# Three edits to the order of loads and sums in a two-layer SwiGLU and attention kernel

## The chip, the cores and the metric

The kernel runs on one core of one Trainium2 chip. The metric is the device time of one execution in microseconds (us). Three executions of the kernel before took 2139.57, 2142.0 and 2146.55 us; the median is 2142.0 us. A further execution was recorded by the hardware profiler, and every row of a profile in this document comes from such a recorded execution.

TensorE is called PE in the profile (PEld is its weight load), VectorE is DVE, ScalarE is ACT, GpSimd is POOL and SyncE, which only issues transfers here, is SP. "L448" is line 448 of the kernel.

## The reference, cut to what matters

One step of an encoder layer over 1024 prompt tokens and 32 sample tokens, 1024 features wide, all in float32:

```python
x = x + 0.5 * swiglu(rms_norm(x, ffn1_norm), ffn1_w_in, ffn1_w_out)   # "layer 0" here
h = rms_norm(x, mix_norm)
# eight stick-breaking attention heads of 64 and four HGRN2 heads of 128 from h @ w_in
sb_o = rms_norm(sb_mix(sq, sk, sv), sb_out_gain)                      # per head
o_h  = rms_norm(o_h, hg_out_gain) * silu(hg)                          # per head
x = x + concat(sb_o, o_h) @ w_out
x = x + 0.5 * swiglu(rms_norm(x, ffn2_norm), ffn2_w_in, ffn2_w_out)   # "layer 1" here

def swiglu(x, w_in, w_out):
    a, b = jnp.split(x @ w_in, 2, axis=-1)        # 1024 -> 2 x 2816
    return (jax.nn.silu(a) * b) @ w_out           # 2816 -> 1024
```

The outputs are the new activations, the new keys and values, and the new HGRN2 states.

## The kernel before, in words

**Stages.** The program is one straight line of instructions in five stages. By the profile's times they are: layer 0's first product (up to 486 us), layer 0's second product (486 to about 700 us), the mixing stage with attention and HGRN2 (to about 1440 us), layer 1's first product (to 1906 us) and layer 1's second product. Every float32 product is made of three passes of PE over a high and a low part of each operand (`PASSES`, `split`), and each feed-forward product is done with seven block products in place of eight (a Strassen-Winograd form). So the weights have to be summed and subtracted (S1 to S4) and split before PE reads them.

**The first product, `first_products`.** It loops over 22 columns `j` of 128 features, and in each over two halves `c` of the tokens (256 and 272 wide). A half is a list of block products `p`, each 12 matmuls on PE into one of eight PSUM banks, followed by an addition on DVE (L591), and for p = 4 and p = 3 a multiplication on POOL (L629 and L625) with a SiLU on ACT between (L624). The first `early` columns (6 in layer 0, 8 in layer 1) have had two of their products done ahead, so their halves have five products, in the order 6, 5, 7, 4, 3. Their parts come back from DRAM in tiles `fp` (`fetch`, L578). While column `j` runs, the weights of column `j + 1` are loaded (`wraw` and `braw`, L469 and L477), summed on DVE (`rS`, L496 to L499) and split in the second half (`S2l`, `S1l`, `S3l`, `A22l`, `S4l`, L159), each right behind the product that last used its buffer. At the end of a half POOL makes a difference `tt` (L563) that SP stores (`td<-tt`, L649), and at the end of a column SP stores `gd<-gt` (L650).

**The sums of the second weights, `out_sums`.** Beside this, once per column in the early columns, at p = 5 of the second half, the kernel loads a raw piece of the second weights in two transfers on SP (`oraw`, L545), makes four sums of it on POOL (`osum`, L549 to L552) and stores them (`sd<-osum`, L553) for the second product. There is one buffer for `oraw` and one for `osum`. The load and the sums stand in `with behind(g, last, stored)`: what SP issues in there comes behind the store of the column before (`stored`), and what POOL does comes behind its last multiplication L629 (`last`).

**The second product, `Second`.** It walks seven products with 11 steps `k` each. Weights come in pieces of two steps: `load_w` issues for each piece a transfer of the raw left operand (`rw`, for p = 1), one of the raw weights (`oraw2`, seen as `oraw`) and whatever `self.bulk` lists for that piece; all of it is issued by SP in that order (`move`, L708). The bulk lists hold the operands of later products: B22 (`qB`, needed from step 12 on) in four parts at pieces 2 to 5, T at 7 to 10, B21 at 12 to 15, and parts of x. `roomy` is false in layer 0 and true in layer 1. The split of a piece is L741 on ACT and L742 on DVE, that of a left operand L756 and L757; the matmuls are L800. The last column's stores go through POOL's own queue (`store = nc.gpsimd`), in both layers.

**The norms in the mixing stage.** `token_factors` squares a head's output, transposes it with PE (`pmc`, L218), sums it on DVE with a tensor_reduce (L219), and takes it to the power -1/2 on POOL (L224, L225). `spread` then widens the factor on ACT (`wide`, L237) and transposes it back with PE (`pb`, L245), and DVE multiplies (L1153 and L1518). PE does the projection of the next heads in between (`pp`, L939).

**What sets the order.** The order of instructions on each engine is not the order of the text. A planner runs through a model of the program and gives each engine the ready instruction with the highest priority; the place in the text is the priority, `high_priority()` raises it, and `behind(...)` fixes an instruction behind another one on the same engine. On the chip every engine then works strictly in that order. The planner doesn't know how long a transfer really takes.

Of the kernel before, what the change touches and what calls it, by code (L numbers as in the profile page):

```python
# [12 lines left out]
ALU = mybir.AluOpType  # L13
AX = mybir.AxisListType
# [6 lines left out]
TP = 1024  # L21
TS = 32
T = TP + TS
GROUPS = ((0, 384), (384, 768), (768, T))
NG = len(GROUPS)
TG = 384
# [181 lines left out]

def token_factors(g, f, psp, sq, w, behind_, tokens=None):


    nc = g.nc
    nb, rows, nh = -(-w // P), min(w, P), f.shape[2]
    mc = psp.tile([P, 3, P], F32, name="pmc", tag="px", bufs=3)
    v = f[0:rows, 0:nb, 0:nh]
    with behind(g, behind_):
        for b in range(nb):
            nc.tensor.transpose(mc[0:rows, b, :], sq[:, b * P:b * P + rows], g.ident)  # L218
    nc.vector.tensor_reduce(out=v.rearrange("p b h -> p (b h)"),  # L219
                            in_=mc[0:rows, 0:nb, :].rearrange("p b (h d) -> p (b h) d", h=nh), axis=AX.X, op=ALU.add)  # L220
    wide = lambda t: t[:, :, None].broadcast_to([rows, nb, nh])
    if tokens is not None:
        nc.gpsimd.tensor_tensor(out=v, in0=v, in1=wide(g.r2[0:rows, tokens]), op=ALU.mult)
    nc.gpsimd.tensor_scalar(out=v, in0=v, scalar1=nh / P, scalar2=EPS, op0=ALU.mult, op1=ALU.add)  # L224
    nc.gpsimd.tensor_tensor(out=v, in0=v, in1=g.mh[0:rows, :, None].broadcast_to([rows, nb, nh]), op=ALU.pow)  # L225
    if tokens is not None:
        nc.gpsimd.tensor_tensor(out=v, in0=v, in1=wide(g.rc[0:rows, tokens]), op=ALU.mult)
# [310 lines left out]

def out_sums(g, pool, w_out, sd, q, h):

    nc = g.nc
    v = w_out[0].rearrange("(f j p) (e d) -> p j f e d", f=2, p=P, e=2)
    raw = pool.get("oraw").rearrange("p (f e d) -> p f e d", f=2, e=2)
    for f in range(2):
        nc.sync.dma_start(raw[:, f], v[:, q, f, :, 256 * h:256 * h + 256])  # L545
    s = pool.get("osum").rearrange("p (i d) -> p i d", i=4)
# [9 lines left out]
def first_products(g, psp, pool, sizes, xs, wts, w_out, gd, td, sd, pd, early, sec, between=None):  # L556
# [3 lines left out]
    stored = added = silu = mm = last = None  # L560
    n_out = 0
    halves = [(q, h) for q in range(FH) for h in range(2)]
# [8 lines left out]
    def fetch(n):  # L571
        j, c = divmod(n, 2)
        if j < early:
# [5 lines left out]
            firsts[j, c] = t  # L579

    for n in range(2):
        fetch(n)
    for j in range(FC):
        n_halves = min(len(halves), j + j // 12 + j // 16 if early < 8 else j + 1 + j // 12)
        gt = gt_of(j)
        store = nc.gpsimd if j == FC - 1 else nc.sync
        for c in range(2):
# [13 lines left out]
            for i, p in enumerate(order):  # L601
# [40 lines left out]
                if (j, c, p) == (FC - 1, 1, 6):  # L642
                    sec.first_weights()
                if p == 5 and n_out < n_halves + c - 1:
                    with behind(g, last, stored):
                        out_sums(g, post, w_out, sd, *halves[n_out])
                    n_out += 1
            sub(tt, gt[:, ROLE[1], cc], tt if j >= FH else gt[:, ROLE[0], cc])
# [10 lines left out]
class Second:  # L659
# [23 lines left out]
    def open(self, psp, qpool, ring, pool, t_first):  # L683
# [15 lines left out]
        for i in range(4):  # L699
            k, e = 3 * i, min(3 * i + 3, FH)  # L700
            for n, at in (("B22", 2), ("T", 7), ("B21", 12)):
                self.bulk[at + i].append((self.q[n][:, k:e], src[n][:, k:e]))
# [436 lines left out]

def sb_out_norm(g, pool, psp, o, w, out):  # L1140
    nc = g.nc
    f = {}

    def factors(c):
# [3 lines left out]
        f[c] = pool.tile([P, 3, 2], F32, name="fo", tag="fo", bufs=3)  # L1148
        token_factors(g, f[c], psp, sq, cw, g.filler)

# [25 lines left out]
def attend_stream(g, m, pool, psp, gi, out):  # L1176
# [87 lines left out]
    while gi == 3 and not m.projected:  # L1264
        yield None
    yield from sb_out_norm(g, pool, psp, o, TP, out)
    m.attended[gi] = True
# [7 lines left out]
def sample_stream(g, m, pool, psp, gi, ck, cv, out):  # L1275
# [66 lines left out]
    while gi == 3 and not m.projected:  # L1342
        yield None
    yield from sb_out_norm(g, pool, psp, os, TS, lambda a, e, o: out(TP, T, o))
    m.sampled[gi] = True
# [61 lines left out]
def hg_stream(g, m, pool, psp, hh, state, outs, out):  # L1407
# [99 lines left out]
    def factors(n):  # L1507
# [5 lines left out]
        fo[n] = pool.tile([P, 3, 1], F32, name="fh", tag="fh", bufs=3)  # L1513
        token_factors(g, fo[n], psp, sq, TG, g.filler)

# [558 lines left out]
```

## Time and profile before

| what | value |
|---|---|
| median of three runs | 2142.0 us (2139.57 to 2146.55) |
| the profiled execution's own time | 2145.02 us |
| its span, first to last instruction | 2143.3 us |
| PE busy in the span | 2101.9 us (98%) |
| DVE, ACT, POOL busy | 1466.2, 935.4, 596.7 us |
| mean share of the granted TensorE clock | 0.999 |

The profiled execution is 3.0 us longer than the median of the runs and lies inside their spread. 1.7 us of its time lie outside the span. A wait in the profile is the idle time of an engine before an instruction, with what ended it. PE has next to none; the other engines are idle for about a third of the span or more.

### The profile page before, as it was taken

What the parts mean: (1) busy time and instruction counts of PE and PEld (TensorE: products, weight loads), DVE (VectorE), ACT (ScalarE), POOL (GpSimd) and SP (SyncE); (2) the same over time, 40 slices, a digit from 0 to 9 for tenths busy, and PEclk for the clock granted to TensorE, in tenths of its full rate; (3) what the DMA queues carried; (4) which work ended last, traced back from release to release, by engine and by line L of the source; (5) the groups of instructions that cost most, each with busy time, mean ns of one, the idle gap of its engine ahead of it and who ended that gap; (6) DMA issues with size and microseconds to landing.
All of it is one profiled execution on the core that took longest, in us unless ns stands there. A gap on an engine that the chain in (4) does not pass through costs nothing. (4 is left out here: it accounts for less than half of the span.)

```text
span 2143.3 us, 41511 instructions
## 1 busy us (share of the span) xinstructions
PE 2101.9 (98%) x16331; PEld 2049.2 (96%) x16331; DVE 1466.2 (68%) x2555; ACT 935.4 (44%) x1830; POOL 596.7 (28%) x878
## 2 busy tenths in 40 slices
PE   8999999999999999999999999999999999999999
PEld 8999999999999999899899898999999999999998
DVE  6776666654678568678678688568667666645775
ACT  6433332324447555564464564245233233334443
POOL 2455554530000201311312311031555454320000
PEclk9999999999999999999999999999999999999999
DMA  7765455538545310111211213555665455566343
GB/s 239 220 206 164 148 166 167 173 126 304 185 129 170 99 44 20 61 54 30 70 42 32 69 54 96 175 170 181 213 192 186 155 173 163 162 228 234 121 145 126
DMA packets 326085, 305.12 MB, mean 142 GB/s; under 512 B 26049, under 2 KB 281793, under 8 KB 325889
## 3 DMA queue, kind: packets, MB, share of 16 engines
q1 hardware_dynamic: 258896, 264.23, 37.9%
q10 hardware_dynamic: 66368, 36.08, 5.9%
q8 instruction: 128, 2.10, 0.4%
q0 software_dynamic: 624, 2.15, 0.3%
q14 instruction: 69, 0.56, 0.1%
HBM read 207.37 MB, written 95.03 MB: 141 GB/s over the span
## 5 line engine op out<-in xcount | busy, mean ns | idle before, releaser
L800 PE MATMUL bk<-tl,wh 128*128 128x256 f32 x1144 | 325.8, 285 | 1.8 <-DVE tl L757 1.8
L800 PE MATMUL bk<-th,wh 128*128 128x256 f32 x1144 | 323.5, 285 | 1.2 <-ACT th L756 1.2
L800 PE MATMUL bk<-th,wl 128*128 128x256 f32 x1144 | 323.0, 283 | 0.0
L939 PE MATMUL pp<-xs_a,wh 128*128 128x384 f32 (+1 forms) x1008 | 258.6, 338 | 0.0
L800 PEld LDWEIGHTS bk<-tl,wh 128*128 128x128 f32 x1144 | 215.7, 189 | 2.5 <-DVE tl L757 2.4
L800 PEld LDWEIGHTS bk<-th,wl 128*128 128x128 f32 x1144 | 216.6, 189 | 0.2 <-issue 0.2
L800 PEld LDWEIGHTS bk<-th,wh 128*128 128x128 f32 x1144 | 214.7, 189 | 1.9 <-ACT th L756 1.7
L939 PEld LDWEIGHTS pp<-xs_a,wh 128*128 128x128 f32 x1008 | 168.6, 189 | 6.0 <-issue 4.1
L939 PE MATMUL pp<-xs_a,wl 128*128 128x384 f32 (+1 forms) x504 | 164.0, 325 | 0.0
L742 DVE SCALAR_TENSOR_TENSOR wl<-oraw,wh 128x1024 fp32r<-128x1024 f32 x78 | 89.3, 1145 | 96.3 <-ACT wh L741 96.3
L624 ACT ACTIVATE gt<-gt 128x256 f32<-128x256 f32 x88 | 37.3, 423 | 261.4 <-DVE gt L591 261.1
L625 POOL TENSOR_TENSOR gt<-gt,b 128x256 f32<-128x256 f32 x88 | 70.8, 804 | 285.4 <-ACT gt L624 285.3
L741 ACT ACTIVATE wh<-oraw 128x1024 fp32r<-128x1024 f32 x78 | 77.7, 996 | 135.7 <-PE bk L800 115.1
L448 PE MATMUL bk<-ops_a,wh 128*128 128x256 f32 (+1 forms) x704 | 130.7, 286 | 2.0 <-ACT e L427 2.0
L159 DVE TENSOR_TENSOR wl<-wraw,wh 128x512 fp32r<-128x512 f32 (+2 forms) x126 | 111.6, 901 | 28.0 <-ACT wh L158 27.7
L158 ACT ACTIVATE wh<-wraw 128x512 fp32r<-128x512 f32 (+2 forms) x126 | 89.5, 731 | 75.4 <-PE pp L939 25.2
L448 PEld LDWEIGHTS bk<-ops_a,wh 128*128 128x128 f32 x704 | 109.0, 188 | 3.2 <-ACT e L427 3.1
L591 DVE TENSOR_TENSOR b<-bk,u 128x272 f32<-128x272 f32 (+1 forms) x176 | 75.4, 428 | 49.1 <-POOL gt L625 26.3
L448 PE MATMUL bk<-ops_a,wl 128*128 128x272 f32 (+1 forms) x352 | 100.0, 285 | 0.2 <-DVE wl L159 0.2
L629 POOL TENSOR_TENSOR gt<-gt,b 128x256 f32<-128x256 f32 x88 | 85.6, 973 | 43.0 <-DVE b L591 32.5
L939 PEld LDWEIGHTS pp<-xs_a,wl 128*128 128x128 f32 x504 | 94.8, 188 | 0.1
L591 DVE TENSOR_TENSOR gt<-bk,p 128x256 f32<-128x256 f32 (+1 forms) x60 | 26.0, 433 | 96.0 <-PE bk L448 91.5
(461 smaller groups left out, 6675.6 us busy)
## 6 DMA issues: line engine op xcount, KB each, us to landing
wraw<-in_ffn_w_in_dram SPq DMA_DIRECT2D x58, 512.0 KB, 4.2
oraw<-in_ffn_w_out_dram SPq DMA_DIRECT2D x94, 256.0 KB, 4.7
sd<-osum SPq DMA_DIRECT2D x44, 512.0 KB, 3.2
gd<-gt SPq DMA_DIRECT2D x42, 528.0 KB, 5.0
braw<-in_ffn_w_in_dram ACTq DMA_DIRECT2D x42, 512.0 KB, 4.6
oraw<-sd SPq DMA_DIRECT2D x40, 512.0 KB, 3.7
oraw<-in_ffn_w_out_dram SPq DMA_DIRECT2D x30, 512.0 KB, 3.7
wraw<-in_w_in_dram SPq DMA_DIRECT2D x28, 512.0 KB, 3.7
```

Source lines behind the costliest of these rows:

```text
L158: high = nc.scalar.activation(hi, src, AF.Copy)
L159: nc.vector.tensor_tensor(out=lo, in0=src, in1=hi, op=ALU.subtract)
L448: mm = g.nc.tensor.matmul(ps, wt[x][:, kk, :], xt[y][:, kk, :], start=(first and kk == 0 and n == 0), stop=(kk == HK - 1 and n == len(PASS ...
L591: add = lambda out, other: nc.vector.tensor_tensor(out=out, in0=ps, in1=other, op=ALU.add)
L624: silu = nc.scalar.activation(gt[:, 1, cc], gt[:, 1, cc], AF.Silu)
L625: nc.gpsimd.tensor_tensor(out=gt[:, 1, cc], in0=gt[:, 1, cc], in1=s["b2"], op=ALU.mult)
L629: last = nc.gpsimd.tensor_tensor(out=gt[:, 0, cc], in0=gt[:, 0, cc], in1=s["b1"], op=ALU.mult)
L741: nc.scalar.activation(h, r, AF.Copy, scale=0.5)
L742: nc.vector.scalar_tensor_tensor(out=l, in0=r, scalar=0.5, in1=h, op0=ALU.mult, op1=ALU.subtract)
L800: nc.tensor.matmul(ps, wt[a][:, d * P:(d + 1) * P], xt[b][:, cols(c)], start=(k == 0 and n == 0), stop=(k == FH - 1 and n == len(PASSES) - 1))
L939: g.filler = nc.tensor.matmul(ps[:, 0:gw(n)], wt[a][:, k, :], xs(b, k)[:, gs(n)], start=(k == 0 and j == 0), stop=(k == KC - 1 and j == le ...
```

## The change

Three edits, and a rewriting of a count.

1. `out_sums` is parted in two: `out_load` (the two transfers L545) and the sums. In layer 1 (`early == 8`) the first piece is loaded ahead of column 0, and those of columns 1 to 7 at p = 7 of the column's first half, outside of `behind`. The sums stay at p = 5 of the second half, behind `last` and `stored`. In layer 0, and from column 8 on, load and sums stay together as before. `due(n)` gives the same number of pieces at each half as the expression that it replaces.
2. In layer 0 the four parts of B22 are listed at pieces 3 to 6, and no longer at 2 to 5. Layer 1 keeps 2 to 5.
3. In `token_factors` the tensor_reduce L219 gets high priority, for the norms of the attention's heads and of the HGRN2 heads of groups 0 to 2; those of group 3 pass `urgent=False`. The factors of q and k had high priority already.

No instruction is added or taken away.

```diff
-def token_factors(g, f, psp, sq, w, behind_, tokens=None):
+def token_factors(g, f, psp, sq, w, behind_, tokens=None, urgent=True):
...
-    nc.vector.tensor_reduce(out=v.rearrange("p b h -> p (b h)"),
-                            in_=mc[0:rows, 0:nb, :].rearrange("p b (h d) -> p (b h) d", h=nh), axis=AX.X, op=ALU.add)
     wide = lambda t: t[:, :, None].broadcast_to([rows, nb, nh])
+    with g.tc.high_priority() if urgent else ExitStack():
+        nc.vector.tensor_reduce(out=v.rearrange("p b h -> p (b h)"),
+                                in_=mc[0:rows, 0:nb, :].rearrange("p b (h d) -> p (b h) d", h=nh), axis=AX.X, op=ALU.add)
...
-def out_sums(g, pool, w_out, sd, q, h):
-
-    nc = g.nc
+def out_load(g, pool, w_out, q, h):
+
     v = w_out[0].rearrange("(f j p) (e d) -> p j f e d", f=2, p=P, e=2)
     raw = pool.get("oraw").rearrange("p (f e d) -> p f e d", f=2, e=2)
     for f in range(2):
-        nc.sync.dma_start(raw[:, f], v[:, q, f, :, 256 * h:256 * h + 256])
+        g.nc.sync.dma_start(raw[:, f], v[:, q, f, :, 256 * h:256 * h + 256])
+    return raw
+
+
+def out_sums(g, pool, raw, sd, q, h):
+
+    nc = g.nc
...
+    def due(n):
+        j, c = divmod(n, 2)
+        return min(len(halves), (j + j // 12 + j // 16 if early < 8 else j + 1 + j // 12) + c - 1)
+
     for n in range(2):
         fetch(n)
+    lead = 2 * early if early == 8 else 0
+    if lead:
+        oraw = out_load(g, post, w_out, *halves[0])
...
-                if p == 5 and n_out < n_halves + c - 1:
+                if p == 5 and n_out < due(2 * j + c):
                     with behind(g, last, stored):
-                        out_sums(g, post, w_out, sd, *halves[n_out])
-                    n_out += 1
+                        if oraw is None:
+                            oraw = out_load(g, post, w_out, *halves[n_out])
+                        out_sums(g, post, oraw, sd, *halves[n_out])
+                    n_out, oraw = n_out + 1, None
+                elif p == 7 and oraw is None and 2 * j + c + 1 < lead and n_out < due(2 * j + c + 1):
+                    oraw = out_load(g, post, w_out, *halves[n_out])
...
-            for n, at in (("B22", 2), ("T", 7), ("B21", 12)):
+            for n, at in (("B22", 2 if self.roomy else 3), ("T", 7), ("B21", 12)):
...
-        token_factors(g, f[c], psp, sq, cw, g.filler)
+        token_factors(g, f[c], psp, sq, cw, g.filler, urgent=urgent)
...
-    yield from sb_out_norm(g, pool, psp, o, TP, out)
+    yield from sb_out_norm(g, pool, psp, o, TP, out, gi < 3)
...
-    yield from sb_out_norm(g, pool, psp, os, TS, lambda a, e, o: out(TP, T, o))
+    yield from sb_out_norm(g, pool, psp, os, TS, lambda a, e, o: out(TP, T, o), gi < 3)
...
-        token_factors(g, fo[n], psp, sq, TG, g.filler)
+        token_factors(g, fo[n], psp, sq, TG, g.filler, urgent=hh < 3)
```

More of the change, by code (lines that the diff above doesn't have):

```diff
@@ L560, in first_products @@
     stored = added = silu = mm = last = None
-    n_out = 0
+    n_out, oraw = 0, None
     halves = [(q, h) for q in range(FH) for h in range(2)]
@@ L579, in fetch @@
             firsts[j, c] = t
+    def due(n):
+        j, c = divmod(n, 2)
+        return min(len(halves), (j + j // 12 + j // 16 if early < 8 else j + 1 + j // 12) + c - 1)
     for n in range(2):
         fetch(n)
+    lead = 2 * early if early == 8 else 0
+    if lead:
+        oraw = out_load(g, post, w_out, *halves[0])
     for j in range(FC):
-        n_halves = min(len(halves), j + j // 12 + j // 16 if early < 8 else j + 1 + j // 12)
         gt = gt_of(j)
@@ L1137, in skewed, with sb_out_norm @@
             yield 0.5
-def sb_out_norm(g, pool, psp, o, w, out):
+def sb_out_norm(g, pool, psp, o, w, out, urgent):
     nc = g.nc
```

## The prediction

> **What bounds the kernel now.** I read the page's busy times first, then PE's waits over the whole execution (total, times, longest, in us), then the chain that ended last.
>
> ```profile
> PE 2101.9 (98%) x16331; PEld 2049.2 (96%) x16331; DVE 1466.2 (68%) x2555; ACT 935.4 (44%) x1830; POOL 596.7 (28%) x878
> ...
> PE bk L448 <- DVE S3l L159: 6.9, 8, 1.6
> PE pb L245 <- ACT wide L237: 4.2, 4, 1.5
> ...
> 1609.26 296.79 PE bk L448 x2446
> ```
>
> PE is the bound. Only time in which it stands still can be won, and what is won reaches the end: the chain's longest piece, 297 us from 1609 us on, is PE alone, so later work just begins earlier. The change takes no instruction away. Each of its three edits is worth the PE idle time that it ends.
>
> **Edit 1, the raw pieces in layer 1.** PE's largest named wait is for S3l, the low part of a summed weight. Windows from one half's first product to the next show its whole cost: the first and last of the six first halves of columns 2 to 7, their sum, and the first half of column 0, which has no stall (length, then busy time and instructions of PE, PEld, DVE, ACT, POOL, granted clock, DMA share, GB/s).
>
> ```profile
> 1522.58:1532.45 9.87, 7.91 (x62) 7.30 (x61) 6.72 (x15) 2.70 (x6) 7.46 (x8) 1.00 0.57 168
> ...
> 1605.40:1613.34 7.94, 7.27 (x62) 7.07 (x61) 6.27 (x14) 1.88 (x3) 5.83 (x7) 1.00 0.67 187
> sum 53.13, PE 45.69 PEld 43.07 DVE 34.89 ACT 11.34 POOL 39.08; mean PE 7.62 PEld 7.18 DVE 5.82 ACT 1.89 POOL 6.51
> ...
> 1493.18:1500.19 7.01, 7.01 (x62) 7.01 (x61) 2.54 (x6) 2.42 (x4) 0.64 (x1) 1.00 1.01 309
> ```
>
> The same matmuls take 53.13 us in six halves and 6 x 7.01 = 42.06 us without a stall: 11.1 us are to be had, more than the wait itself, since PE's pipe also fills anew. The chain up to the last of these stalls names the cause; the rows of POOL and SP (start, length) show where the load stands, and a group of POOL what it costs there.
>
> ```profile
> 1597.56 4.73 DMA oraw<-in_ffn_w_out_dram
> 1602.36 0.74 POOL osum L551
> ...
> 1607.08 0.71 POOL gt L625
> ...
> 1608.60 0.61 DVE S3l L159
> ...
> 1590.44 0.74 POOL L552 TENSOR_TENSOR osum<-oraw,osum 128x256 f32<-128x256 f32 x1
> 1598.36 0.74 POOL L629 TENSOR_TENSOR gt<-gt,b 128x256 f32<-128x256 f32 x1 [1.20 <-DVE b L591]
> ...
> 1593.09 0.43 SPq L553 DMA_DIRECT2D sd<-osum  x1
> 1596.00 0.33 SPq L650 DMA_DIRECT2D gd<-gt  x1
> ...
> L551 POOL TENSOR_TENSOR osum<-oraw 128x256 f32<-128x256 f32 x6 | 4.4, 739 | 26.8 <-DMA oraw<-in_ffn_w_out_dram 26.8
> ```
>
> POOL has done L629 at 1598.36 + 0.74 = 1599.10 and stands before the first sum until 1602.36, with L625 of the first half behind it in its queue; DVE needs L625 (it frees the buffer b), and S3l is behind that on DVE. POOL waits so in each of the six columns: 26.8 us, 4.5 on average, 3.3 here, in the mildest. The load is late because it is held behind the store gd at 1596.00, though its buffer came free with the last sum before, at 1590.44 + 0.74 = 1591.18.
>
> After the change only that buffer holds it. The store of the sums (1593.09) needs the same release; I put the two transfers right behind it, at 1593.5, so that they land 4.7 us later, at 1598.2, before POOL is ready. This presumes that the planner takes a load ahead of stores that are older in the text. It does so now:
>
> ```profile
> 1499.50 0.84 SPq L578 DMA_DIRECT2D fp<-pd  x1
> ...
> 1509.90 0.64 SPq L649 DMA_DIRECT2D td<-tt  x1
> ```
>
> The fetch at 1499.50 is from the text of column 1, the store after it from column 0. So the sums, L625 and S3l come 3.3 us earlier here and 4.5 on average, and what has to be beaten is 7.94 - 7.01 = 0.9 us here and 9.87 - 7.01 = 2.9 at most. What the two transfers are moved past (gd, td, the fetches and the weights behind them on SP) comes about 1.5 us later, by the estimate of two issues of 0.7 us (fp's takes 0.84); it is wanted half a column, 7 us, later. The piece ahead of column 0 stands among that column's fetches; a late fetch there is covered by eight PSUM banks, at 7.01 / 5 = 1.4 us a product. Bounds: all 11.1 us, or nothing if the load stays behind gd. Nearest is the row of the buffer's release: I take **-10 us**.
>
> The four sums will now run beside DVE's sums rS. Of POOL's groups of one shape, this one takes longest against the 739 ns above:
>
> ```profile
> L549 POOL TENSOR_TENSOR osum<-oraw 128x256 f32<-128x256 f32 x6 | 7.2, 1206 | 0.9 <-DMA oraw<-in_ffn_w_out_dram 0.9
> ```
>
> The Trainium skill speaks against the edit here: by "SBUF — State Buffer", section "Who interferes with whom", a DVE instruction with two SBUF inputs and a GpSimd instruction that reads SBUF block one another. The two rows agree with it in kind. If all four sums grew from 739 to 1206 ns, 1.9 us of the 3.3 would be gone in the mildest column; 1.4 would still beat 0.9, and an estimate with one such stall left makes this edit -9 and the whole sum -15.5.
>
> **Edit 2, B22 in layer 0.** The rows of SP, POOL and PE at the start of the second product, SP's wait there, the transfers by kind (KB, us to landing), and two windows.
>
> ```profile
> 487.81 0.42 SPq L708 DMA_DIRECT2D qB<-gd  x1
> 497.52 0.36 SPq L708 DMA_DIRECT2D rw<-gd  x1
> ...
> 487.95 0.58 POOL L650 DMA_DIRECT2D gd<-gt  x1
> ...
> 504.78 0.39 PE L800 MATMUL bk<-th,wh 128*128 128x256 f32 x1 [1.21 <-ACT th L756]
> 506.12 0.58 PE L800 MATMUL bk<-tl,wh 128*128 128x256 f32 x1 [0.96 <-DVE tl L757]
> ...
> SPq L708 <- DMA gd<-gt: 9.2, 1, 9.2
> ...
> qB<-gd SPq DMA_DIRECT2D x2, 792.0 KB, 9.1
> gd<-gt POOLq DMA_DIRECT2D x1, 528.0 KB, 9.5
> ...
> 503.00:506.00 3.00, 0.96 (x6) 0.54 (x4) 1.78 (x3) 2.12 (x3) 0.00 (x0) 0.98 1.04 390
> 506.00:509.40 3.40, 3.28 (x15) 3.28 (x16) 0.68 (x2) 0.18 (x1) 0.00 (x0) 0.51 1.04 414
> ```
>
> SP can't issue piece 3 (its rw at 497.52) before the store gd, issued at 487.95, has landed, 9.5 us later; the first part of B22 goes out just ahead of that store and shares the engines with it. PE then waits for piece 3: 1.21 + 0.96 = 2.17 us, and after that the clock is granted at 0.51 for 3.40 us, a loss of 3.40 x 0.49 = 1.67 us. Together 3.8 us.
>
> Behind the edit that part is issued after piece 3. Its 811 KB (792 x 1024 bytes) take 2.0 us at the 414 GB/s of the last row, so the store lands, and piece 3 starts, some 2.0 us earlier. That leaves about 0.2 us of the 2.17, too little for the clock to drop. But piece 4 queues behind the same bytes as now and comes only those 2 us earlier, while PE would come 3.8 earlier: I leave 0.8 us for a new short wait there. The last part of B22 now comes at piece 6, ahead of piece 7's weights, 541 KB or 1.3 us at the same rate; this is the bound on the other side. I take **-3 us** (-3.8 to +1.3), nearest to the store's row.
>
> The Trainium skill's "TensorE: Matmul & The Clock Gate", Part 1, has the clock at half only after an idle window of about 3.4 us. By that, 2.17 us of waiting cost no clock, and edit 2 would be worth some 1.4 and the sum -15. The window's 0.51 disagrees, and decides.
>
> **Edit 3, the norms' sums.** One of three alike places, at the end of group 2's heads, on PE, DVE, POOL and ACT, and PE's waits of that kind from 890 to 1230 us, which hold the ends of groups 0 to 2.
>
> ```profile
> 1210.96 0.71 PE L218 MATMUL pmc<-identr,sq 128*128 128x128 f32 x5
> ...
> 1211.69 1.27 DVE L1109 TENSOR_TENSOR_SCAN t<-t,left,zero 64x512 f32<-64x512 f32 x1
> ...
> 1213.94 0.40 DVE L219 TENSOR_REDUCE fo<-pmc 128x4 f32<-128x256 f32 x1
> ...
> 1215.05 1.61 POOL L225 TENSOR_TENSOR fo<-fo,mh 128x4 f32<-128x4 f32 x1
> ...
> 1216.70 0.42 ACT L237 ACTIVATE wide<-fo 128x256 f32<-128x256 f32 x1 [3.93 <-POOL fo L225]
> ...
> 1217.17 0.44 PE L245 MATMUL pb<-identr,wide 128*128 128x128 f32 x2 [1.27 <-ACT wide L237]
> ...
> PE pb L245 <- ACT wide L237: 4.0, 3, 1.5
> ```
>
> The transposes end at 1211.67, the sum L219 starts at 1213.94, behind the sample's scan and other work; POOL, ACT and PE follow it in a chain with no slack. Ahead of the scan it starts up to 2 us earlier, behind the scan 1 us; PE's wait here is 1.27 us. The three waits of this kind are 4.0 us (the fourth of the first fence is in group 3, which is left as it was). I take **-3.5 us**. Behind the raised sums the scan comes up to two sums later, 2 x 0.40 us; if PE had to wait for that in all three places, it would cost 2.4 us. Range -4.0 to +2.4; I count nothing for the raised sums elsewhere.
>
> **The sum.** -10 - 3 - 3.5 = -16.5 us. The profiled execution took 2145.02 us and would take 2128.5; it lies 3.0 us over the median of the runs, so the median goes from 2142.0 to **2125.5 us**.
>
> **The rivals.** *The load stays behind gd*, because the planner's own times put SP's stores first; for it speaks that SP is often in the text's order, against it the fetch at 1499.50. Edits 2 and 3 alone: 2142.0 - 6.5 = 2135.5 us. *The raised sums cost more than they give:* +2.4 for edit 3 in place of -3.5: 2142.0 - 10.6 = 2131.4. For it speaks that DVE is busy without a break around the place shown, against it that PE's next use of the scan is far behind. *Slower:* SP works strictly in order, and the pulled-forward transfers may stand on SP waiting for their buffer while fetches and weights queue behind them; then the addition of a half comes late for want of fp. That decides from where the delay exceeds the 7 us of a half. If each of the 14 halves of columns 1 to 7 then lost as much as the worst now (2.9), it would be 14 x 2.9 = 40.6, less 6.5 from the other edits: 2142.0 + 34 = 2176 us. Against it: the store of the sums already makes SP wait for the same release. *A wash:* a new plan of the mixing stage gives back on PE, in new short waits, what edits 2 and 3 win, and half of edit 1 stays: 2142 - 5 = 2137.
>
> **How the numbers follow.** Forecast 0.66, the load unmoved 0.10, the raised sums at a loss 0.10, a wash 0.09, slower 0.05. A measurement tells 0.3% (6.4 us) from no change, so "faster" is below 2135.6. Forecast and raised sums lie there, and half of the unmoved load: 0.66 + 0.10 + 0.05, less 0.01 for the forecast's weak end, is 0.80. The same 0.05 + 0.09 + 0.01 = 0.15; slower 0.05. The best end is all three bounds, -11.1 - 3.8 - 4.0 = -18.9, from a median that may itself lie at the lowest run's 2139.57: 2120. The other end takes in the unmoved load and the wash: 2138. The forecast's own range is 2120 to 2131.
>
> **What would show it.** In the changed trace: oraw issued ahead of gd in columns 1 to 7, no wait of POOL L551 for DMA there, halves of 7.0 to 7.3 us and no wait for S3l; rw of piece 3 about 2 us earlier after the last store, no window at a clock of 0.5; L219 ahead of or right behind the scan and waits for `wide` under 1 us in all. Wrong I would be if the halves kept near 8 us or more, if new waits of PE for fp, rS or the scan's result came up, or if the gd store took its 9.5 us without B22 beside it.

## The result and the profile after

Run in turn with the kernel before, the changed kernel took 2136.56 us, the median of six runs (2134.30 to 2139.93); the kernel before took 2143.18 us, the median of its six (2139.57 to 2146.55). The ratio is 0.997 with a 95% interval of 0.9956 to 0.9984, a gain of 6.4 us (3.4 to 9.4). The forecast was a gain of 16.5 us, to 2125.5. The direction was right; the gain is two fifths of the forecast.

The profiled execution after took 2135.5 us, with a span of 2133.8 us. First the page's busy times, then the longest of PE's waits in the whole span (in all, times, longest, us).

```profile
PE 2100.4 (98%) x16331; PEld 2048.8 (96%) x16331; DVE 1469.5 (69%) x2555; ACT 936.5 (44%) x1830; POOL 600.7 (28%) x878
```

```profile
PE bk L872 <- DVE dg L860: 7.6, 1, 7.6
PE bk L816 <- DVE tl L773: 2.7, 4, 1.5
PE pb L246 <- POOL fh L226: 1.8, 4, 0.7
PE bk L449 <- DVE S1l L159: 1.6, 2, 1.0
...
PE bk L449 <- DVE S2l L159: 1.3, 2, 1.1
PE pb L246 <- ACT wide L238: 1.2, 4, 0.4
```

The wait for `dg` stands ahead of PE's first instruction. It took 7.8 us before, and no edit touches it; it was the largest there too, so the prediction's "PE's largest named wait is for S3l" holds only for the waits behind it. Of these the largest before were 6.9 us for S3l and 4.2 us for `wide`. S3l is down to 0.5, all of it in layer 0, and `wide` to 1.2. S1l, S2l and `fh` have grown. The line numbers of this kernel are one or two higher than before up to the sums rS (the norms' sum L219 is L221, rS is L497 to L500), 6 to 12 higher from the sums of the raw piece to the last multiplication (L549 is L555, a product's addition L591 is L603, the silu L624 is L636, the multiplications L625 and L629 are L637 and L641), and 16 higher behind that (L800 is L816).

**Layer 1.** The six first halves of columns 2 to 7, in the windows that the prediction used (length, then busy time of PE, PEld, DVE, ACT, POOL, granted clock, DMA share, GB/s):

```profile
1520.90:1528.08 7.18, 7.18 (x63) 7.14 (x62) 6.17 (x15) 2.15 (x5) 4.84 (x5) 1.00 0.77 220
...
1595.96:1604.33 8.37, 7.35 (x63) 7.15 (x62) 8.03 (x15) 3.01 (x5) 4.90 (x5) 1.00 0.67 207
sum 45.05, PE 43.77 PEld 42.96 DVE 39.72 ACT 14.91 POOL 29.50; mean PE 7.30 PEld 7.16 DVE 6.62 ACT 2.48 POOL 4.92
```

They fell from 53.13 to 45.05 us. But two halves outside this list grew: the first of column 1 from 7.33 to 8.45, the second of column 3 from 7.53 to 8.26. All 15 halves, from the first product of column 0 to that of column 7's second half, took 120.16 us before (1493.18 to 1613.34) and 113.96 after (1490.36 to 1604.32): -6.2 us, of the 10 forecast. Without a stall they take 108.8, as six kernels below show. The waits of POOL and DVE in these columns, after:

```profile
POOL osum L555 <- DMA oraw<-in_ffn_w_out_dram: 2.9, 1, 2.9
...
DVE rS L497 <- DMA braw<-in_ffn_w_in_dram: 22.5, 8, 3.8
```

POOL's wait for the raw piece is gone but for column 0 (26.8 us in six columns before). In its place DVE waits for `braw`, 22.5 us instead of the 10.4 of before:

```profile
DVE rS L496 <- DMA braw<-in_ffn_w_in_dram: 10.4, 7, 2.6
```

**Layer 0.** The store gd at the start of the second product lands (its data have arrived) 6.5 us after its issue instead of 9.5 (first row, from the transfers by kind), and the two waits at 504.78 and 506.12 with the half clock behind them are gone. One wait has come up, in the next of the seven products (second row, from PE's timeline):

```profile
gd<-gt POOLq DMA_DIRECT2D x1, 528.0 KB, 6.5
```

```profile
526.48 0.39 PE L816 MATMUL bk<-tl,wh 128*128 128x256 f32 x1 [1.51 <-DVE tl L773]
```

From 486 to 657 us of its profile, first product to last, this stage is 2.25 us shorter than before.

**The mixing stage** is 0.7 us shorter, of the 3.5 forecast: 1.3 at the second of the three places, 0.1 or less at the first and the third, and 0.7 lost again at the end of group 3's heads. Start, early products and layer 1's second product make up the rest of the 9.5 us between the two profiled executions; the medians lie 6.6 us apart.

### The profile page after: what moved, and what is told of

Same layout as the page of the kernel before. It is cut to its first block, busy times and chain, and to the rows that moved or that the text cites. A ratio compares the mean times of both kernels' runs of the same rounds, so it can differ in the third digit from the quotient of the medians.

```text
span 2133.8 us, 41508 instructions
## 1 busy us (share of the span) xinstructions
PE 2100.4 (98%) x16331; PEld 2048.8 (96%) x16331; DVE 1469.5 (69%) x2555; ACT 936.5 (44%) x1830; POOL 600.7 (28%) x878
## 5 line engine op out<-in xcount | busy, mean ns | idle before, releaser
L816 PE MATMUL bk<-tl,wh 128*128 128x256 f32 x1144 | 325.2, 285 | 2.4 <-DVE tl L773 2.4
L816 PE MATMUL bk<-th,wh 128*128 128x256 f32 x1144 | 323.0, 284 | 0.0
L816 PE MATMUL bk<-th,wl 128*128 128x256 f32 x1144 | 322.5, 282 | 0.0
L816 PEld LDWEIGHTS bk<-tl,wh 128*128 128x128 f32 x1144 | 215.1, 188 | 3.0 <-DVE tl L773 3.0
L816 PEld LDWEIGHTS bk<-th,wl 128*128 128x128 f32 x1144 | 216.0, 189 | 0.2 <-issue 0.2
L816 PEld LDWEIGHTS bk<-th,wh 128*128 128x128 f32 x1144 | 214.1, 188 | 0.5 <-ACT th L772 0.2
L637 POOL TENSOR_TENSOR gt<-gt,b 128x256 f32<-128x256 f32 x88 | 72.4, 823 | 307.1 <-ACT gt L636 307.1
L636 ACT ACTIVATE gt<-gt 128x256 f32<-128x256 f32 x88 | 37.3, 424 | 245.7 <-DVE gt L603 245.4
L641 POOL TENSOR_TENSOR gt<-gt,b 128x256 f32<-128x256 f32 x88 | 86.0, 977 | 46.7 <-DVE b L603 35.7
L603 DVE TENSOR_TENSOR b<-bk,u 128x272 f32<-128x272 f32 (+1 forms) x176 | 75.3, 428 | 32.9 <-PE bk L449 19.2
L603 DVE TENSOR_TENSOR gt<-bk,p 128x256 f32<-128x256 f32 (+1 forms) x60 | 25.9, 432 | 98.1 <-PE bk L449 95.0
```

The source lines that it names most:

```text
L603: add = lambda out, other: nc.vector.tensor_tensor(out=out, in0=ps, in1=other, op=ALU.add)
L636: silu = nc.scalar.activation(gt[:, 1, cc], gt[:, 1, cc], AF.Silu)
L637: nc.gpsimd.tensor_tensor(out=gt[:, 1, cc], in0=gt[:, 1, cc], in1=s["b2"], op=ALU.mult)
L641: last = nc.gpsimd.tensor_tensor(out=gt[:, 0, cc], in0=gt[:, 0, cc], in1=s["b1"], op=ALU.mult)
L816: nc.tensor.matmul(ps, wt[a][:, d * P:(d + 1) * P], xt[b][:, cols(c)], start=(k == 0 and n == 0), stop=(k == FH - 1 and n == len(PASSES) - 1))
```

## The experiments

Each kernel was timed in turn with the kernel before on one chip; the last of them, without the scan, was profiled only. Ratios are to the kernel before, with a 95% interval; 0.1% is 2.1 us. Stage times come from one profiled execution each, and the table shows how much they change from one execution to another where the code of the stage is the same (layer 0: 486 to 657 us; layer 1: the 15 halves).

| kernel | ratio (interval) | layer 0's second product, us | layer 1's 15 halves, us |
|---|---|---|---|
| before | 1 | 172.2 | 120.2 |
| edit 1 alone | 0.9983 (0.9974 to 0.9991) | 172.2 | 115.9 |
| edit 2 alone | 0.9999 (0.9990 to 1.0008) | 170.1 | 118.5 |
| edit 3 alone | 0.9994 (0.9986 to 1.0003) | 170.3 | 118.7 |
| all three | 0.9970 (0.9956 to 0.9984) | 170.0 | 114.0 |
| wraw half a column early | 0.9965 (0.9953 to 0.9976) | 170.1 | 115.9 |
| wraw early with priority | 0.9976 (0.9967 to 0.9985) | 170.1 | 115.7 |
| S2h ahead of the silu | 0.9957 (0.9944 to 0.9971) | 172.1 | 115.2 |
| three of four sums cut | 0.9943 (0.9927 to 0.9959) | 170.0 | 108.8 |
| raw loads cut | 0.9940 (0.9924 to 0.9956) | 171.2 | 108.8 |
| no pieces early | 0.9938 (0.9925 to 0.9951) | 170.0 | 108.8 |
| no pieces early, x later | 0.9937 (0.9924 to 0.9951) | 169.4 | 108.8 |
| no pieces early, edits 2 and 3 undone | 0.9950 (0.9938 to 0.9963) | 171.9 | 108.8 |
| no pieces early in both layers | 0.9961 (0.9948 to 0.9975) | 170.3 | 108.8 |

### The three edits, each alone

The other two edits are taken out again: `lead = 0` takes out edit 1, `("B22", 2)` edit 2, no `high_priority()` around the sum edit 3.

> Edit 1 alone on the kernel before: the early load of the raw pieces, without the two other edits. Theory A (each edit acts in its own stage, so the gains add): the 15 half-columns of layer 1 take 114.0 us as in the changed kernel's profile (120.2 before), the other stages are as before; time 6 us below before, 2137. Theory B (the edits help each other, since layer 1's start and its buffers depend on what came ahead): halves between 115 and 118 us, time 2 to 4 us below. In both DVE's rS waits for braw's transfer over 20 us in all (8.0 before) and braw lands 6.7 to 7.5 us after its issue.

> Edit 2 alone: layer 0's B22 parts one piece later. Theory A: the stage of layer 0's second product from 486 to 657 us is 2.2 us shorter than before, with a new wait of PE for tl about 1.5 us long at 526 and no window with the clock at 0.5; time 2 us below before, 2141. Theory B (the new wait at 526 came from another edit or from that one execution): no wait there, the stage 4 us shorter, time 2139.

> Edit 3 alone: the norms' sums with priority in groups 0 to 2. Theory A: the mixing stage is 0.5 to 1 us shorter than before, with PE's waits for wide and fh at the three places near 0.2 to 0.6 us each instead of 1.2 to 1.5; time 1 us below before, 2142. Theory B (as predicted, 3.5 us): time 2139.5.

Times: 2140.86, 2144.73 and 2143.02 us against 2144.38 for the kernel before. By the ratios edit 1 gives 3.6 us (1.9 to 5.6), edit 2 nothing that can be told (0.2, within 1.9 either way), edit 3 1.3 us (-0.6 to 3.0). The sum is 5.1, beside 6.4 measured for all three at once: they add within their uncertainty. Edit 1's term of 10 is thus the one that failed most. (For edit 1 alone the figures are those of theory B, 115.9 us and 3.5 us by the medians; but the spread told of next explains them, without help of the edits for each other.)

Two things in the table were not expected. Layer 1's halves differ by 1.7 us between three executions of the same code (120.2, 118.5, 118.7), and by 2.4 between four with edit 1 (114.0 in the changed kernel, 115.9 with edit 1 alone, and 115.9 and 116.4 in two kernels below that leave the order of this stage as it is, the early `wraw` and the one without the scan). The means are 119.1 and 115.5: edit 1 is worth 3.6 us there, as in the times, not the 6.2 of the first pair of profiles. And with B22 at its old place layer 0's second product took 172.2, 172.2 and 171.9 us in three executions, each with the stall at 504 and a clock near a half behind it, but 170.3 in the profile of edit 3 alone, where that stall did not come: the store landed in 8.0 us, and the window in which the clock had been 0.51 shows it at 1.00.

```profile
506.00:509.40 3.40, 3.40 (x31) 3.40 (x30) 0.00 (x0) 1.05 (x2) 0.00 (x0) 1.00 1.04 411
```

With B22 one piece later the stage takes 170.0 to 170.7 us in eight executions and 171.2 and 172.1 in two. The means are 171.7 with the old place and 170.5 with the new. So edit 2 takes away a stall that comes in three executions of four, and leaves a shorter one at 526 (0.8 to 1.8 us). Theory A holds for the new wait in kind (0.8 us in that run), not for the time; the gain is 1.2 us in the mean, too little for the times to tell. In the slowest of the ten (172.1, "S2h ahead of the silu") the new wait was 1.81 us, and the next 4.0 us (527.1 to 531.1) had the clock at 0.61, so the new place doesn't rule the slow clock out either.

### Layer 1: what is late behind edit 1

The rows of the ACT queue and of DVE, ACT and PE show one stall of the changed kernel, at the start of a column:

```profile
1539.39 0.37 ACTq L478 DMA_DIRECT2D braw<-in_ffn_w_in_dram  x1
...
1546.87 0.78 DVE L497 TENSOR_TENSOR rS<-braw 128x512 f32<-128x512 f32 x1 [3.48 <-DMA braw<-in_ffn_w_in_dram]
...
1549.96 0.74 ACT L609 ACTIVATE gt<-fp 128x256 f32<-128x256 f32 x2 [9.19 <-DMA gd<-gt]
1550.60 0.61 ACT L158 ACTIVATE S2h<-rS 128x512 fp32r<-128x512 f32 x1
...
1551.25 0.69 DVE L159 TENSOR_TENSOR S2l<-rS,S2h 128x512 fp32r<-128x512 f32 x1 [0.99 <-ACT S2h L158]
...
1551.27 0.39 PE L449 MATMUL bk<-ops_a,S2h 128*128 128x256 f32 x1 [0.57 <-ACT S2h L158]
```

`braw` lands 7.5 us after its issue; rS waits 3.48 us for it. S2h, which PE wants at 1550.7, stands behind a silu that waits for the store gd to land. Both transfers are late. Another stall comes at one place in all six profiles of kernels that have edit 1 and leave out none of its loads and sums: in the first half of column 7 PE waits 1.0 to 1.1 us for S1l, and the half takes 8.4 to 8.8 us. In the changed kernel rS has waited 2.65 us for `braw` there, and DVE then splits `wl` for column 8 between S2l and S1l:

```profile
1595.81 1.76 DVE L159 TENSOR_TENSOR wl<-wraw,wh 128x1024 fp32r<-128x1024 f32 x1
...
1598.76 0.39 PE L449 MATMUL bk<-ops_a,S1l 128*128 128x256 f32 x1 [1.02 <-DVE S1l L159]
```

The first theory (A) was that `braw` shares the DMA engines with what edit 1 has moved beside it; the rival (B) that DVE is slowed beside POOL's sums, or held by its own order. A first try moved `wraw`, the other half of the weights:

```diff
+                if c == 1 and i == 0 and lead and j + 2 <= early: wts.load_a(j + 2)
...
-                            wts.load_a(j + 1)
+                            if not (lead and 2 <= j + 1 <= early): wts.load_a(j + 1)
```

> The changed kernel, with the load of layer 1's first half of the input weights (wraw, columns 2 to 8) issued half a column earlier, so that it no longer travels beside braw. Theory A (braw lands late because fp, wraw, td and gd share the DMA engines with it, and everything behind rS on DVE is late): braw lands in at most 5.8 us instead of 6.7 to 7.5, DVE's wait of rS for it falls from 22.5 us to under 10, PE's waits for S2l and S1l in columns 2 to 7 go, halves 114.0 -> 111 to 112 us, time 2 to 3 us below the changed kernel (2134). Theory B (rS is late because DVE runs beside POOL's sums, or because of DVE's own order): braw may land sooner, but the halves stay at 113.5 to 114.5 and the time within 1 us. Theory C (wraw now shares with the raw pieces instead): POOL's sums wait for DMA again, over 8 us in all, and the halves go up to 116 or more.

2137.77 us, halves 115.9 us. It tells nothing of the theories: the planner put `wraw` where it had been, 0.3 to 0.8 us ahead of `braw` and behind the store of td. So it is a repeat of the changed kernel, and counted as one above. With priority (`with g.tc.high_priority()` around the load) it does go earlier:

> The changed kernel with wraw of columns 2 to 8 half a column early and with priority on SP's queue, so that it goes out ahead of the store of td, behind the store of the sums, some 3 us before braw. Theory A (braw shares the DMA engines): braw lands in 5.5 to 6.3 us instead of 6.7 to 8, halves 111 to 113 us against 114 to 116, time 2 us below the changed kernel. Theory B (DVE beside POOL): braw sooner, halves within 1 us of the changed kernel's 114 to 116. Theory C (it only moves the sharing to the raw pieces): POOL's sums wait for their transfer, halves 116 or more.

2139.65 us, halves 115.7; `braw` lands in 7.7 us in the median. SP's rows of this kernel show why:

```profile
1534.40 0.38 SPq L470 DMA_DIRECT2D wraw<-in_ffn_w_in_dram  x1
1537.42 0.33 SPq L666 DMA_DIRECT2D td<-tt  x1
1537.81 1.20 SPq L545 DMA_DIRECT2D oraw<-in_ffn_w_out_dram  x2
1539.12 1.11 SPq L584 DMA_DIRECT2D fp<-pd  x2
```

`wraw` left, and the raw piece of the same 512 KB took its place beside `braw` (issued at 1539.1). That fits theory A's mechanism, but its forecast failed: the expectation had the raw pieces' sharing as theory C, but it is `braw` that is late, not the sums. Two cuts then took the sums and the raw loads away. For the sums, `if cut: nc.gpsimd.memset(s[:, 1:4], 0.0)` replaces three of the four; for the loads the first piece's buffer is kept:

```diff
-                    n_out, oraw = n_out + 1, None
+                    n_out, oraw = n_out + 1, oraw if j + 1 < early == 8 else None
```

> The changed kernel, in layer 1's columns 0 to 7 with three of the four sums of a piece left out and one memset of zeros in their place (so those sums of the output weights are missing from the output); all transfers stay. Theory A (transfers share the DMA engines): braw still lands in 6.5 to 8 us, halves 113 to 116, time within 1.5 us of the changed kernel. Theory B (POOL's sums beside DVE slow rS and the low parts): no rS over 0.75 us, S1l and S3l at 0.68, halves 109 to 111, time 4 us below.

> The changed kernel, in layer 1's columns 1 to 7 with the raw pieces' loads left out (the sums are made again and again from the first piece, so the sums of the other pieces are wrong); sums and stores stay. That takes 512 KB of some 3.3 MB per column off the DMA engines. Theory A: braw lands in 5 to 6.3 us, DVE's wait for it falls by 10 us or more, halves 110 to 112, time 3 us below the changed kernel. Theory B: halves stay at 113 to 116, since the sums still run beside DVE.

2132.14 and 2131.84 us, and both without any stall in the 15 halves: 108.8 us, lower than either theory had said. The median times of `braw` to landing in the same columns: before, changed kernel, sums cut, raw loads cut.

```profile
braw<-in_ffn_w_in_dram ACTq DMA_DIRECT2D x5, 512.0 KB, 5.1
```

```profile
braw<-in_ffn_w_in_dram ACTq DMA_DIRECT2D x6, 512.0 KB, 7.0
```

```profile
braw<-in_ffn_w_in_dram ACTq DMA_DIRECT2D x6, 512.0 KB, 6.1
```

```profile
braw<-in_ffn_w_in_dram ACTq DMA_DIRECT2D x6, 512.0 KB, 5.2
```

The cut of the loads decides against B as the only cause. There DVE's sums rS, 25 of 32 of them beside POOL's sums, are the slowest of all these kernels (changed kernel: 955 and 759 ns), and PE doesn't wait:

```profile
L499 DVE TENSOR_TENSOR rS<-wraw,braw 128x512 f32<-128x512 f32 x8 | 9.2, 1156 | 0.0
L498 DVE TENSOR_TENSOR rS<-rS,wraw 128x512 f32<-128x512 f32 x8 | 8.4, 1055 | 0.3
```

Its wait for `braw`, 22.5 us in the changed kernel, is down to a quarter:

```profile
DVE rS L497 <- DMA braw<-in_ffn_w_in_dram: 5.5, 6, 1.6
```

The cut of the sums was expected by A to change nothing, and it removed the stalls as well, as B had forecast. `braw` landed sooner there too, in 6.1 us and not in the 6.5 to 8 that A expected. Its rows show why only in part: `wraw` still travels with `braw` (1.3 us ahead of it) and the store of the sums has landed before `braw` goes out, as in the changed kernel, but a fetch of 272 KB goes out some 4 to 5 us ahead of `braw` and no longer 1.2. So DVE beside POOL's sums probably has a share in the stalls. Without sums `braw` may take 6.1 us (here) or 6.7 (into column 1 of the kernel without early pieces, below) and PE doesn't wait; with them, in edit 1 alone, 6.4 us go with a first half of 7.6 us in column 1. No run separates the shares. What the two cuts show is that the sums alone make no stall, and that with the loads gone none is left.

Nor does one landing time decide. In edit 1 alone `braw` took 6.9 to 8.0 us ahead of columns 4 to 6, and their first halves are at 7.01 to 7.03; PE had lost 4.6 us around column 2 just before. How much a late `braw` costs depends on the slack that earlier stalls have left.

What was still open is which of the two late landings sets S2h: `braw`, or gd by way of the silu ahead of S2h on ACT. One swap on ACT alone tells them apart (the order on PE, DVE, POOL and SP stays as it was):

```diff
-                nc.scalar.activation(gt[:, 0, cc], t[:, 1], AF.Silu)
+                with behind(g, s2 if early == 8 else None): nc.scalar.activation(gt[:, 0, cc], t[:, 1], AF.Silu)
...
-                        wts.split(j + 1, wn)
+                        s2 = (wts.split(j + 1, wn), s2)[wn != "S2"]
```

> The changed kernel with one swap on ACT alone in layer 1's early columns: S2h, the high part of the next column's first weight, ahead of the silu of the fetched product (gt<-fp), which waits until the store gd of two columns before has landed; the order on PE, DVE, POOL and SP is the same. Theory G (in the changed kernel S2h stands on ACT behind that silu, so the late landing of gd, 5.6 us in the median, sets it in most columns, and braw only in some): S2h starts within 0.8 us of the sum rS it reads, PE's waits for S2h go, halves 110 to 112.5 us, time 2 to 3 us below the changed kernel. Theory B' (braw alone sets it through rS; gd lands in its shadow): S2h moves by 0.3 us at most, halves 113.5 to 116, time within 1 us. Against both: the silu, now behind S2h, may bring S1h late, with halves over 116.

2137.39 us, halves 115.2 us, within the 114.0 to 116.4 of the changed order. S2h now starts 0.1 us behind the sum that it reads, and PE still waits, in this execution (the slowest of its five) most of all in column 2, where `braw` took 11.8 us to land:

```profile
PE bk L449 <- ACT S2h L158: 1.5, 1, 1.5
PE bk L449 <- DVE S2l L159: 1.3, 1, 1.3
PE bk L449 <- DVE S1l L159: 1.1, 1, 1.1
```

The halves speak against theory G: with gd out of S2h's way, about as much stall is left, so gd's landing was mostly in the shadow of `braw`'s. The times don't settle it: the ratio, 0.9957, is 2.8 us below the changed kernel's, and the intervals overlap.

What edit 1 did to the queue is read from SP's rows of one column, before and after:

```profile
1537.14 0.39 SPq L469 DMA_DIRECT2D wraw<-in_ffn_w_in_dram  x1
1544.46 0.33 SPq L649 DMA_DIRECT2D td<-tt  x1
1544.84 0.43 SPq L553 DMA_DIRECT2D sd<-osum  x1
1545.37 1.74 SPq L578 DMA_DIRECT2D fp<-pd  x2
```

```profile
1532.65 1.53 SPq L545 DMA_DIRECT2D oraw<-in_ffn_w_out_dram  x2
1537.74 0.33 SPq L665 DMA_DIRECT2D td<-tt  x1
1538.17 0.38 SPq L584 DMA_DIRECT2D fp<-pd  x1
1538.60 0.49 SPq L470 DMA_DIRECT2D wraw<-in_ffn_w_in_dram  x1
```

Before, `wraw` went out ahead of td and 8.9 us ahead of `braw` (issued 1546.0); in five of these columns it was 8.1 to 8.9 us. After, the raw piece has that place, `wraw` stands behind td, which waits on SP for POOL's `tt`, and goes out 0.8 us ahead of `braw`. The DMA engines are full in both cases while `braw` is under way, before (1562.2, the `braw` of a column) and after (1555.4); the length of the window is its time to landing, and there is more to move:

```profile
1562.20:1567.30 5.10, 4.93 (x42) 4.73 (x41) 3.02 (x8) 0.95 (x2) 3.19 (x4) 1.00 1.05 313
```

```profile
1555.40:1562.10 6.70, 6.70 (x57) 6.70 (x56) 2.99 (x7) 0.95 (x2) 5.09 (x7) 1.00 1.04 321
```

5.1 us at 313 GB/s are 1.6 MB, 6.7 us at 321 are 2.2 MB: the 0.5 MB between them are as much as `wraw`, which had landed 4.4 us ahead of `braw`'s issue before (1553.5 + 4.3) and was issued 0.8 us ahead of it after. The packets in the two windows bear this out. `wraw` moves in packets of 512 bytes: on SP's queue there are none before, and 1024 after, all of it. The rest of that queue moves 1.1 MB in both.

### The pieces out of the early columns

If the pieces' transfers are the trouble, they can go where columns last 20.4 us instead of 14.6:

```diff
-        return min(len(halves), (j + j // 12 + j // 16 if early < 8 else j + 1 + j // 12) + c - 1)
+        return min(len(halves), j + j // 12 + j // 16 + c - 1 if early < 8 else max(0, 2 * j + c + 1 - 2 * early))
...
-    lead = 2 * early if early == 8 else 0
+    lead = 0
```

> The changed kernel with no piece at all in columns 0 to 7 of layer 1; columns 8 to 18 do two pieces each instead (one per half-column, loaded and added in place as there before). All work is still done. Theory A and B alike (what is left of the stalls comes from the pieces, by their transfers or by their sums): the 15 half-columns fall to 109 to 110 us (7.02 and 7.54 each). If POOL's second piece per column is hidden in columns 8 to 18, time 5 us below the changed kernel (2133 against about 2138); if POOL, waiting 4.5 us for each piece's transfer, comes late with its products there, those columns grow by up to 0.5 us per half, 11 us in all, and the time is 2144. Theory C (the stalls are DVE's own order and have nothing to do with the pieces): halves stay at 114 to 116.

2131.97 us, 13 us below the kernel before and, by the medians and by the ratios, 5 to 7 below the changed one. The 15 halves are at 7.01 to 7.02 and 7.53 to 7.54 us. In columns 8 to 18 POOL waits far more for the pieces, but its work there is not on the path: the halves from column 7's second on take 285.0 us in all, as in every kernel here.

```profile
POOL osum L557 <- DMA oraw<-in_ffn_w_out_dram: 71.9, 20, 7.8
```

This beats both kernels. It keeps edits 2 and 3; without them, and so with nothing of edit 1 either:

> The kernel before with its pieces moved out of layer 1's columns 0 to 7 alone, that is without edits 2 and 3. Theory A (edits 2 and 3 are worth what the stage times of the profiles show, 0.3 to 2.1 us for edit 2 by the execution and 1.2 us for edit 3): layer 1's halves 109.0 us, mixing stage 1.2 us longer than with edit 3, time 2 to 3 us above the 2132 with them, 2134 to 2135. Theory B (they are worth nothing): 2132.

2134.60 us, 2.6 above, though the intervals of the two ratios overlap. Edit 1's whole 10 us are thus there (0.9950 is 10.7 us), but by moving the pieces away, not by loading them earlier. The same in layer 0, `return min(len(halves), max(0, 2 * j + c + 1 - 2 * early))` for both:

> The kernel with no pieces in layer 1's columns 0 to 7, with the same done in layer 0: none in its columns 0 to 5, two per column from column 6. In layer 0 POOL waits 17.7 us for five pieces' transfers in columns 1 to 5 and PE's halves there stand up to 0.9 us over their shortest. Theory (the same cause in both layers): all halves of layer 0's columns 1 to 5 at 7.02 and 7.50 us, no wait of PE for S3l or S4l there, time 2 us lower, 2130. Rival (in layer 0 the two pieces per column come beside the first products' constants and transfers of later columns): the early halves shrink, but halves of 10.06 and 10.31 grow by as much; time 2132.

2137.11 us, 5 us slower than with layer 1 alone. The early columns of layer 0 did as expected: the halves up to column 5's first take 79.7 instead of 82.7 us. But in column 9 the second piece met POOL's building of masks, which the kernel makes beside these columns. DVE's copy of a mask waited for POOL, and the addition that PE needed stood behind it on DVE (rows of DVE and PE, then the window behind the wait):

```profile
232.12 0.66 DVE L95 CAST cmask<-mtmp 128x128 fp32r<-128x128 f32 x1 [7.46 <-POOL mtmp L92]
...
235.68 0.59 PE L449 MATMUL bk<-T2s,S2h 128*128 128x272 f32 x1 [4.91 <-DVE gt L603]
```

```profile
235.60:239.50 3.90, 3.82 (x17) 3.82 (x18) 3.87 (x7) 0.42 (x1) 3.74 (x4) 0.50 0.01 5
```

4.9 us of wait and 3.9 us at half the clock (2.0 us lost) give back more than the 3.0 that the early columns won.

### Layer 0's new wait, and the norms

> The kernel with no pieces in layer 1's columns 0 to 7 (2132 us), with in addition layer 0's first four transfers of x issued four pieces later (pieces 8 to 11 instead of 4 to 7; 541 KB each). Theory A (from 495 to 525 us the DMA engines are full, 0.96 to 1.04 of their time, so moving B22 only changes which transfer comes late; bytes have to leave the stretch): the wait of PE for tl at 526 (1.4 to 1.6 us with edit 2) goes, layer 0's second product takes 168.3 instead of 170.0 us, time 1.5 us lower, 2130.5. Theory B (the weights' two buffers set the pace, each load waits for wl two pieces back): the wait stays at 1.3 us or more, time as before the edit, 2132.

`self.bulk[(4 if self.roomy else 8) + i]` in place of `self.bulk[4 + i]`. The wait at 526 went, as theory A said, but another of 0.8 us came at 495, and the stage took 169.4 us in place of 170.0. The time, 2132.14, is the same. The 0.6 us are too few to be told from the spread of that stage.

> The changed kernel with the samples' scan on DVE (64x512, 1.26 us) left out and a copy on ACT in its place, so that the attention of the samples is not the reference's. Theory A (edit 3 gives back at the first and the third place, since POOL's power of a sum, 0.85 us alone, takes 1.80 us beside the scan that now runs next to it): the power takes 0.85 us there, and PE's three waits at 904 to 907 us and at 1212 to 1215 us, 1.2 us at each place, fall to under 0.5 in all. Theory B (POOL's order is the limit: copies and memsets of other streams stand between): the waits stay at 1 us or more per place.

In the changed kernel POOL's power of a sum takes twice as long at the first place, where the scan runs on DVE beside it (rows of POOL and DVE), as at the second:

```profile
902.18 1.80 POOL L226 TENSOR_TENSOR fh<-fh,mh 128x3 f32<-128x3 f32 x1
...
902.07 1.26 DVE L1125 TENSOR_TENSOR_SCAN t<-t,left,zero 64x512 f32<-64x512 f32 x1
...
1057.17 0.85 POOL L226 TENSOR_TENSOR fh<-fh,mh 128x3 f32<-128x3 f32 x1
```

Without the scan it takes 0.85 us there. PE's waits fell only at the third place (1.22 to 0.76 us); at the first they are 1.24 in place of 1.19. From well before to well behind the place, PE is 0.4 us faster than in the changed kernel at the first and 0.2 at the third, so the scan accounts for a part at most. As the planner had also changed PE's order, this run doesn't settle what sets the waits.

## Why the prediction was wrong in size

**Edit 1 is the term that failed: -10 forecast, -3.6 timed (-1.9 to -5.6), -6.2 in the first pair of profiles.** Its first steps held. The planner put the load right behind the store of the sums, POOL's wait and the stall on S3l went. The step that failed is the sentence that what the two transfers are moved past "comes about 1.5 us later" and is wanted "half a column, 7 us, later". For the fetches that was near enough. For `wraw` it was not a matter of 1.5 us: its place on SP changed from ahead of td to behind it, from 8.9 us ahead of `braw` to 0.8. `wraw` itself came in time, but its 512 KB now travel with `braw`, and `braw` had no such margin. It landed in 7.0 us instead of 5.1, and rS, S2h, S2l and S1l followed. With the raw loads left out `braw` is back at 5.2 us and no stall is left, though the sums still run beside DVE. I had looked at when each transfer is wanted, and not at which bytes would share the engines with the transfer that had the least slack. DVE's wait for it, 10.4 us in these columns of the profile before, was not among the rows that I quoted.

**The step on DVE beside POOL** came true in kind (rS up to 1.2 us). By itself it makes no stall: the cut of the raw loads has it worst and has none. Whether it adds to the stalls behind a late `braw` is open, since the cut of the sums has none either; the prediction's -10 put it at nothing. The estimate by the Trainium skill's "SBUF — State Buffer", section "Who interferes with whom", put one stall at 1 us for it. The runs show the slowing that the section names (this sum 684 ns before, 1156 in that run), but no stall that it makes alone.

**Edit 2, -3 forecast:** -2.25 in the first pair, and nothing that the timed runs can tell. The steps held in kind: store 3 us sooner, no half clock, a short new wait behind the same bytes. In the first pair the term that was mis-sized is that wait, 1.5 us where I had left 0.8. In the mean of the executions (1.2 us) the starting point failed too: of four executions with the old order one had 1.2 us of waits and no half clock in place of the 3.8 us. And the new wait can be longer, up to 1.8 us.

**Edit 3, -3.5 forecast, -0.7 in the profiles, -1.3 timed (-3.0 to +0.6):** the step "PE's wait here is 1.27 us" counted the wait for `wide` as won in all three places. The sums did come earlier, and the waits for `wide` went from 4.2 to 1.2 us. But with DVE no longer the latest, PE waits for other links: at the first and the third place 1.2 us of waits are left, for `fh`, `wide` and a POOL instruction. POOL's power runs beside the scan there (1.80 for 0.85 us), but without the scan 1.24 us are left at the first, so what holds these two places is not shown. Only at the second place were the 1.3 us won. The group 3 end, which the edit leaves as it was, changed by more (203.7 to 205.3 us from profile to profile).

**The rivals.** The slower one, that SP's order makes fetches and weights late, named the right queue and the wrong damage: the weights weren't late for their own use, they made another transfer late, at (115.5 - 108.8) / 8 = 0.8 us per column and not 5.8. The nearest is the wash, half of edit 1 and nothing of the others (2137 us), which was given 0.09. Its reason, waits in the mixing stage, is only half of what happened, so that its number came so near is luck. Of the signs that I named for being wrong, "new waits of PE for fp, rS or the scan's result" was the one that came: PE's new waits are for S2h, S2l and S1l, the parts of rS.

## What to carry to other kernels

A transfer that is moved earlier takes a place on a queue and on the DMA engines. Before counting its gain, list what it displaces and then which transfer with little slack the displaced bytes now meet; the wait to look for in the profile before is the second one on the same path (here DVE's for `braw`), since it becomes the first. Where the work can go to a stage with slack, that beats a better place in the full one, but look there too for what stands in the same in-order queues, as the masks in layer 0 did. And where a term rests on one stall in one profile, a second profile of the same code is worth having first.

## What was not expected of the hardware

**The clock after a short wait.** The same pattern of waits did not always bring the half clock. With edit 1 alone, 1.28 and 1.26 us of waits in layer 1 (PE busy 1.74 of 3.00 us) were followed by 3.2 us at 0.51. In the kernel that asks for `wraw` half a column early, whose order here is the changed kernel's, PE was busy only 0.55 of 3.00 us at that place, and the clock stayed at 1.00 (the first two rows are of the one kernel, the next two of the other):

```profile
1524.40:1527.40 3.00, 1.74 (x13) 1.54 (x14) 3.00 (x8) 1.98 (x4) 1.81 (x2) 0.95 0.02 8
1527.40:1530.60 3.20, 3.20 (x17) 3.20 (x17) 2.62 (x7) 0.80 (x2) 1.72 (x3) 0.51 0.52 134
```

```profile
1521.10:1524.10 3.00, 0.55 (x3) 0.30 (x2) 3.00 (x6) 1.99 (x5) 0.24 (x1) 1.00 0.44 153
1524.40:1527.40 3.00, 3.00 (x26) 3.00 (x27) 3.00 (x7) 0.95 (x2) 1.79 (x3) 1.00 0.13 44
```

So the idle time by itself doesn't decide it; what does was not found.

**One code, different landings.** `braw` of column 2 took 6.9 and 7.5 us to land in two profiles of the changed order and 10.4 to 11.8 in three others. Stages that hang on a full set of DMA engines changed by 1.7 to 2.4 us from execution to execution, each part of the mixing stage ahead of group 3's end by 0.4 us or less.
